# A two-layer decoder trunk: input projections by Strassen's seven products, results passed to the next phase through DRAM

## The chip, the core and the metric

The kernel runs on one core of a Trainium2 chip. The core has five engines that each work through their own list of instructions in order: TensorE (PE) for matrix products, with weight loads (PEld) beside them; VectorE (DVE) and ScalarE (ACT) for elementwise work, both of which read PSUM, the memory that PE writes; GpSimd (POOL) for elementwise work in SBUF, the on-chip memory; and SyncE (SP), which here issues all DMA transfers between DRAM and SBUF. An instruction that waits for a semaphore holds up everything behind it on its engine. The metric is the device time of one execution in microseconds (us).

## The reference, cut to what matters

The input is 1024 tokens of width 1024 in float32. Layer 0 is retention with 4 heads, layer 1 is stick-breaking attention with 8 heads. Both multiply their normed input with wide weight matrices first (`proj`, `kv`), and both end in an output projection, a norm and a residual sum.

```python
u = rms_norm(h, ret_norm_pre[i]); proj = u @ ret_w_in[i]        # 1024 x 1024 @ 1024 x 6144
q, k, v, g = jnp.split(proj, [1024, 2048, 4096], axis=-1)
q = rope(split_heads(q, 4), pos); k = rope(split_heads(k, 4), pos) * 256 ** -0.5
o = retention_chunkwise(q, k, v)          # decayed causal scores, a carried state
o = (o - mu) * lax.rsqrt(var + EPS)       # per head
o = merge_heads(o).astype(h.dtype) * jax.nn.silu(g)
y = o @ ret_w_out[i]
h = h + rms_norm(y, ret_norm_post[i])
kv = rms_norm(h, kv_norm) @ w_kv                                # 1024 x 1024 @ 1024 x 3072
u = rms_norm(h, sb_norm_pre[j]); proj = u @ sb_w_in[j]          # 1024 x 1024 @ 1024 x 3072
o = stick_breaking_attention(q, k_shared, v_shared)             # A = sigmoid(z) * prod(1 - sigmoid(z))
y = (merge_heads(o) * jax.nn.silu(g)) @ sb_w_out[j]
h = h + rms_norm(y, sb_norm_post[j])
```

So the input projections are a 1024 x 1024 matrix times 1024 x 12288 in all.

## The kernel before, in words

Activations are held transposed, channels on the 128 partitions and tokens along the free axis. Every matrix product is done in a format of reduced precision (`F32R`), three times over: an operand is split into a high and a low part, and `mm3` (L114 to L117) adds high x high, high x low and low x high in one PSUM bank. The split (`unit` L107 to L111, `split` L216 and L217) is a copy on ACT into the reduced format and a subtraction on DVE.

`run` (L691) goes through four phases: layer 0 for tokens 0 to 511, layer 0 for tokens 512 to 1023, then layer 1 for each half (`AHead` and `CPair` with t = 0 and 1). Within a phase there are four units (a retention head, or a pair of stick-breaking heads). A unit has three input projections (`proj`, L119: 16 steps of 6 matmuls of 512 columns each, 96 matmuls), its attention (`scores` and `mix`, or `rows` and `mix`), a gate, and its output projection (`outproj`, L145). Weights are loaded and split once per phase, so twice in all. The output of a projection is read by DVE and ACT straight from PSUM and stays in SBUF until its attention uses it. The value and the retention gate come out with tokens on the partitions, because there the activation tile is the stationary operand of the matmul; the queries and keys come out with channels on the partitions.

The order of the work around the change is written out by hand: `merge` (L172) puts the steps of side lists between the steps of a main list, so that score, transpose and mixing matmuls of one unit stand between projection matmuls of the same or the next unit. `merge(H.gproj(), (H.mix(), 3, 0), ...)` in L729 is one such line, `merge(P.kqproj(), (st + [gate], 6, 2), ...)` in L738 another. The norms before the projections are not applied to the activation but to what comes out (`X.cos`, `X.col`, `X.rows`), so the first matmul needs only one tile of x and one of weights. A planning tool then orders instructions on each engine by their dependencies and hands out the buffers.

The seam between layers is spread in the same way: the post-norm of one half (`a_post`, L421) runs beside the projections of the next half, and the last unit's output projection stands beside the loads for the next phase.

Of the kernel before, what the change touches and what calls it, by code (L numbers as in the profile page):

```python
# [15 lines left out]
D = 1024  # L16
# [4 lines left out]
VD = 512  # L21
# [5 lines left out]
G_PRE, G_POST, G_KV, G_SB, G_SBPOST = range(5)  # L27


@with_exitstack  # L30
def trunk(ctx, tc, xT, wts, gains, trig, ident_in, cols, out):
# [7 lines left out]
    BUFS = dict(xh=8, y=8, tab=2, wraw=3, whl=3, qk=4, v=4, vo=4, oT=4, A=5, sgn=2, AT=3,  # L39
                ko=2, sg=4, row=1, f2=5, acc=2, small=24, col=8, mm=4, z=2, o=2)  # L40
    cnt = [0]

    def S(tag, shape, dt=F32):
        cnt[0] += 1
        return sb.tile([128] + list(shape), dt, tag=tag, name=f"{tag}{cnt[0]}", bufs=BUFS[tag])

# [7 lines left out]
    def hl(tag):  # L54
        return S(tag, [2, 512], F32R)
# [8 lines left out]

# [26 lines left out]
    def unit(idx, gain=None):  # L91

        raw = S("wraw", [1024])
        if idx:
            dma(raw[:], wts[idx])
        else:
            gain = [(0, 512, None), (512, 1024, None)]
            for a, b, _ in gain:
                dma(raw[:, a:b], wts[idx, :, a:b])
        w = S("whl", [2, 1024], F32R)  # L100
        if gain is None:
            pieces = [(0, 1024, None)]
        else:
            pieces = gain
        for a, b, g in pieces:
            if g is None:
                A_.activation(w[:, 0, a:b], raw[:, a:b], AF.Copy)  # L107
                V.tensor_tensor(w[:, 1, a:b], raw[:, a:b], f32(w[:, 0, a:b]), ALU.subtract)  # L108
            else:
                A_.activation(w[:, 0, a:b], raw[:, a:b], AF.Copy, scale=g)  # L110
                V.scalar_tensor_tensor(w[:, 1, a:b], raw[:, a:b], g, f32(w[:, 0, a:b]), ALU.mult, ALU.subtract)  # L111
        return w

    def mm3(p, lh, ll, rh, rl, start, stop):  # L114
        MM(p, lh, rh, start=start, stop=False)  # L115
        MM(p, lh, rl, start=False, stop=False)  # L116
        MM(p, ll, rh, start=False, stop=stop)  # L117

    def proj(base, xh, typ, evac, gain=None):  # L119


        box = {}

        def chunk(j):
            i, half = divmod(j, 2)
            kk, c = divmod(i, 2)
            if j == 0:
                box["b"] = [PS("mm") for _ in range(4)]
            if j % 4 == 0:
                box["w"] = unit(base + kk, gain(kk) if gain else None)  # L130
            w, x, banks = box["w"], xh[i], box["b"]
            for b in (2 * half, 2 * half + 1):
                bl = slice(128 * b, 128 * b + 128)
                if typ == "N":
                    n = slice(512 * c + 128 * b, 512 * c + 128 * b + 128)
                    mm3(banks[b][:], w[:, 0, n], w[:, 1, n], x[:, 0, :], x[:, 1, :], i == 0, i == 7)
                else:
                    n = slice(512 * c, 512 * c + 512)
                    mm3(banks[b][:], x[:, 0, bl], x[:, 1, bl], w[:, 0, n], w[:, 1, n], i == 0, i == 7)
            if j == 15:  # L140
                evac(banks)

        return [lambda j=j: chunk(j) for j in range(16)]

    def outproj(base, oT, y, first, acc=None, tag="mm"):  # L145

        box = {}

        def chunk(j):
            c, half = divmod(j, 2)  # L150
            ng, b = divmod(c, 2)
            if j % 4 == 0:
                box["w"] = unit(base + ng)
# [6 lines left out]
            if half == 0:  # L160
                return
# [672 lines left out]
```

## Time and profile before

| | us |
|---|---|
| Time, median of 3 runs | 1819.01 (1818.63 to 1819.77) |
| The profiled execution's own time | 1819.82 |
| Its span, first to last instruction | 1818.0 |
| PE busy | 1767.5 (97%), 8290 matmuls |
| DVE busy | 1038.1 (57%) |
| ACT busy | 724.1 (40%) |
| POOL busy | 308.6 (17%) |
| DMA | 208.09 MB, mean 114 GB/s |

A row of the profile's groups reads: line, engine, operation, output tile and input tiles by the program's names, shape, number of instructions, then after the bar the time that they were busy and the mean of one in nanoseconds, then the idle time of that engine ahead of them and what ended it. Matmuls overlap: the next one starts before the last one's recorded end, so the duration of one (about 390 ns for 512 columns) is longer than the pace at which they follow each other, and the pace is read from the start times in the timeline. The table of waits says which engine waited for which instruction, how long in total, how often, and how long at most. In a table of windows, each stretch of time has the busy time of each engine with the number of instructions, and the clock that was granted to PE (1.00 is full).

### The profile page before, as it was taken

To read this page: it belongs to the slowest core of one execution; us is meant where nothing else is said; L and a number is where in the kernel's file an instruction comes from. 1 tells how busy PE (TensorE), PEld (TensorE's weight loads), DVE (VectorE), ACT (ScalarE), POOL (GpSimd) and SP (SyncE) were. 2 spreads that over 40 slices of the span, in tenths; PEclk is the share of its full clock that TensorE was granted. 3 is DMA by queue.
4 is the path that set the end of the run, shared out by engine and by line. 5 is a ranking of instruction groups with operands and counts; after the bars stand their busy time and mean duration, and the time that the engine had idled before them with its cause. 6 is when DMAs were issued, how large, how long until landed. Compare 5 with 4: busy or idle time off the path is not lost.

```text
span 1818.0 us, 21852 instructions
## 1 busy us (share of the span) xinstructions
PE 1767.5 (97%) x8290; PEld 1466.5 (81%) x8290; DVE 1038.1 (57%) x1588; ACT 724.1 (40%) x1288; POOL 308.6 (17%) x376
## 2 busy tenths in 40 slices
PE   7999999999899999999999999999998999999987
PEld 6888888888788888888877888888876887887876
DVE  7363454564945363545596465556586446756665
ACT  4343323353333232323454343443444434444441
POOL 4110010113431010111122120201212012101123
PEclk9999999999999999999999999999999999999999
DMA  5222222343362232243364423354244232222321
GB/s 175 82 94 92 93 82 92 108 158 105 136 212 93 70 105 92 83 147 108 116 245 172 140 72 127 115 180 133 99 133 134 87 105 93 92 82 91 108 79 49
DMA packets 66376, 208.09 MB, mean 114 GB/s; under 512 B 7520, under 2 KB 9696, under 8 KB 66272
## 3 DMA queue, kind: packets, MB, share of 16 engines
q1 hardware_dynamic: 66272, 206.70, 33.9%
q8 instruction: 65, 1.06, 0.2%
q14 instruction: 39, 0.32, 0.1%
HBM read 173.12 MB, written 33.55 MB: 114 GB/s over the span
## 4 chain that ended last, share of the span: by engine, by line
PE 71%; issue 17%; DVE 7%; POOL 2%; DMA 2%; ACT 1%; SPq 0%; POOLq 0%; DVEq 0%; ACTq 0%
PE pmm L115 19%; PE pmm L117 19%; PE pmm L116 19%; PE po L117 3%; PE po L116 3%; PE po L115 3%; DVE sgn L550 2%; DMA tab<-h 1%; DVE whl L111 1%; PE pz L117 1%; PE pz L116 1%; PE pz L415 1%; PE pz L115 1%; PE pz L575 1%; DVE A L551 1%
## 5 line engine op out<-in xcount | busy, mean ns | idle before, releaser
L108 DVE TENSOR_TENSOR whl<-wraw,whl 128x1024 fp32r<-128x1024 f32 (+1 forms) x158 | 196.6, 1246 | 217.6 <-ACT whl L107 217.3
L115 PE MATMUL pmm<-xh,whl 128*128 128x512 f32 x768 | 308.3, 401 | 11.5 <-ACT whl L107 7.3
L115 PE MATMUL pmm<-whl,xh 128*128 128x512 f32 x768 | 302.1, 394 | 4.1 <-DVE v L308 2.7
L117 PE MATMUL pmm<-xh,whl 128*128 128x512 f32 x768 | 301.9, 393 | 0.7 <-DVE whl L108 0.7
L116 PE MATMUL pmm<-xh,whl 128*128 128x512 f32 x768 | 300.9, 392 | 0.0
L116 PE MATMUL pmm<-whl,xh 128*128 128x512 f32 x768 | 300.3, 391 | 0.0
L117 PE MATMUL pmm<-whl,xh 128*128 128x512 f32 x768 | 300.3, 391 | 0.0
L107 ACT ACTIVATE whl<-wraw 128x1024 fp32r<-128x1024 f32 (+1 forms) x158 | 165.3, 1047 | 237.9 <-PE pmm L117 225.6
L111 DVE SCALAR_TENSOR_TENSOR whl<-wraw,gn,whl 128x256 fp32r<-128x256 f32 (+1 forms) x256 | 153.2, 639 | 103.5 <-ACT whl L110 103.0
L110 ACT ACTIVATE whl<-wraw,gn 128x256 fp32r<-128x256 f32 (+1 forms) x256 | 143.7, 608 | 148.7 <-PE pmm L117 111.0
L115 PEld LDWEIGHTS pmm<-xh,whl 128*128 128x128 f32 x768 | 145.3, 189 | 41.4 <-ACT whl L107 7.3
L115 PEld LDWEIGHTS pmm<-whl,xh 128*128 128x128 f32 x768 | 144.9, 189 | 34.1 <-DVE v L308 2.9
L117 PEld LDWEIGHTS pmm<-xh,whl 128*128 128x128 f32 x768 | 144.8, 189 | 33.5 <-DVE whl L108 1.7
L117 PEld LDWEIGHTS pmm<-whl,xh 128*128 128x128 f32 x768 | 144.7, 188 | 30.8
L116 PEld LDWEIGHTS pmm<-whl,xh 128*128 128x128 f32 x768 | 145.0, 189 | 28.3
L116 PEld LDWEIGHTS pmm<-xh,whl 128*128 128x128 f32 x768 | 145.3, 189 | 26.6
L548 POOL TENSOR_SCALAR_AFFINE_SELECT sgn<-sgn 128x128 f32<-128x128 f32 x64 | 24.9, 389 | 638.8 <-ACT sgn L543 603.0
L115 PE MATMUL pmm<-oT,whl 128*128 128x512 f32 x336 | 132.9, 395 | 0.0
L117 PE MATMUL pmm<-oT,whl 128*128 128x512 f32 x336 | 131.5, 391 | 0.0
L116 PE MATMUL pmm<-oT,whl 128*128 128x512 f32 x336 | 131.4, 391 | 0.0
L550 DVE TENSOR_TENSOR_SCAN sgn<-sgn 128x128 f32<-128x128 f32 (+3 forms) x64 | 92.7, 1448 | 58.8 <-POOL sgn L548 58.8
L191 POOL TENSOR_TENSOR acc<-acc,f 128x512 f32<-128x512 f32 x49 | 74.4, 1522 | 147.5 <-ACT f L190 146.6
(182 smaller groups left out, 2822.5 us busy)
## 6 DMA issues: line engine op xcount, KB each, us to landing
wraw<-in_wts_dram SPq DMA_DIRECT2D x254, 512.0 KB, 3.3
xh<-hh SPq DMA_DIRECT2D x16, 512.0 KB, 3.7
v<-v SPq DMA_DIRECT2D x16, 512.0 KB, 3.2
vo<-v SPq DMA_DIRECT2D x32, 256.0 KB, 3.2
st<-ko SPq DMA_DIRECT2D x8, 512.0 KB, 3.6
vo<-in_xT_dram SPq DMA_DIRECT2D x16, 256.0 KB, 5.1
ko<-st SPq DMA_DIRECT2D x8, 512.0 KB, 3.9
h<-y SPq DMA_DIRECT2D x16, 256.0 KB, 2.7
```

Source lines behind the costliest of these rows:

```text
L107: A_.activation(w[:, 0, a:b], raw[:, a:b], AF.Copy)
L108: V.tensor_tensor(w[:, 1, a:b], raw[:, a:b], f32(w[:, 0, a:b]), ALU.subtract)
L110: A_.activation(w[:, 0, a:b], raw[:, a:b], AF.Copy, scale=g)
L111: V.scalar_tensor_tensor(w[:, 1, a:b], raw[:, a:b], g, f32(w[:, 0, a:b]), ALU.mult, ALU.subtract)
L115: MM(p, lh, rh, start=start, stop=False)
L116: MM(p, lh, rl, start=False, stop=False)
L117: MM(p, ll, rh, start=False, stop=stop)
L191: G.tensor_tensor(acc[:], acc[:], t[:], ALU.add)
L415: nc.tensor.transpose(pt[:, 128 * e:128 * e + 128], on[:, 128 * e:128 * e + 128], ident[:])
L548: G.affine_select(n[:, dg], n[:, dg], [[-1, 128]], ALU.is_gt, 1.0, base=0, channel_multiplier=1)
L550: V.tensor_tensor_scan(n[:, :W][:, ::-1], n[:, :W][:, ::-1], n[:, :W][:, ::-1], 1.0, ALU.mult, ALU.bypass)
L551: V.tensor_tensor(a[:, :W - 1], a[:, :W - 1], n[:, 1:W], ALU.mult)
```

## The change

The four phases become five stages in a row. (1) All of layer 0's input projections, over all 1024 tokens. (2) Retention of the four heads, with the output projection of the head before between its steps. (3) The norms and the residual sum for both halves of the tokens. (4) All of layer 1's input projections. (5) Stick-breaking attention of the four pairs, with the output projection of the pair before between its steps, and the end. What a projection gives goes to DRAM and is loaded again by the attention stage.

The projections are done in blocks. The activation matrix (channels by tokens) is cut into 2 x 2 blocks of 512 channels by 512 tokens; for every 256 output columns, the weights are cut into 2 x 2 blocks of 512 channels by 128 columns. Seven products of sums of such blocks, in the Winograd form of Strassen's algorithm, replace the eight plain ones: `XOps` makes the seven activation operands, `Pair` makes the seven weight operands (`one` and `two` split one or two blocks with one copy on ACT and one subtraction on DVE, 512 or 1024 wide) and runs the products `p1` to `p7`, 12 matmuls of 512 columns each. `project` runs `p1` and `p2` of four pairs first, beside the preparation of the operands that need the second half of the tokens (`second`), then `p5`, `p6`, `p3`, `p7` and `p4` of these four, and then the other pairs whole. A `Pair` covers both halves of the tokens, and there are 24 of them in each layer. The sums need a normed activation, so the norm now stands ahead of the first product. Every projection now comes out with channels on the partitions, and the values are transposed on PE (`PutV`).

The core of the diff:

```diff
+NB, NHALF = 46, 16
...
-def trunk(ctx, tc, xT, wts, gains, trig, ident_in, cols, out):
+def trunk(ctx, tc, xT, wp, wo, gains, trig, ident_in, cols, out):
-    BUFS = dict(xh=8, y=8, tab=2, wraw=3, whl=3, qk=4, v=4, vo=4, oT=4, A=5, sgn=2, AT=3,
-                ko=2, sg=4, row=1, f2=5, acc=2, small=24, col=8, mm=4, z=2, o=2)
+    BUFS = dict(b=NB, h=NHALF, small=24, col=8, mm=4, z=2, o=2)
...
-    def proj(base, xh, typ, evac, gain=None):
...
+    class XOps:
+        def put(self, name, kt, src):
+            x = self.o[name][kt] = hl("x" + name)
+            split((x[:, 0, :], x[:, 1, :]), src)
+        def first(self, kt):
+            self.put("B11", kt, self.src[kt][:, 0, :])
+            self.put("B21", kt, self.src[4 + kt][:, 0, :])
+        def second(self, kt):
+            a, b = self.src[kt], self.src[4 + kt]
+            b11, b12, b21, b22 = a[:, 0, :], a[:, 1, :], b[:, 0, :], b[:, 1, :]
+            t1 = N("t1", [512])
+            V.tensor_tensor(t1[:], b12, b11, ALU.subtract)
+            self.put("T1", kt, t1[:])
+            V.tensor_tensor(b11, b22, t1[:], ALU.subtract)
+            self.put("T2", kt, b11)
+            self.put("B22", kt, b22)
+            G.tensor_tensor(b12, b22, b12, ALU.subtract)
+            self.put("T3", kt, b12)
+            G.tensor_tensor(b21, b21, b11, ALU.subtract)
+            self.put("T4", kt, b21)
+    class Pair:
+        def prep_s12(self):
+            r0, r1 = self.raw
+            s = N("s", [2, 4, 128])
+            V.tensor_tensor(s[:, 0], r0[:, 1], r1[:, 1], ALU.add)
+            V.tensor_tensor(s[:, 1], s[:, 0], r0[:, 0], ALU.subtract)
+            self.s2 = s
+            self.two(("S1", "S2"), s[:])
...
+        def p1(self, tag="mm"):
+            self.al = PS(tag)
+            self.mul(self.al, "A11", "B11", True)
+            self.c1 = self.copy(self.al, "c")
+        def p2(self, tag="mm"):
+            p = PS(tag)
+            self.mul(p, "A12", "B21", True)
+            self.consume(0, 0, self.plus(self.c1, p))
+        def p5(self, tag="mm"):
+            self.be = PS(tag)
+            self.mul(self.be, "S1", "T1", True)
+            self.c5 = self.copy(self.be, "c")
+        def p6(self):
+            self.mul(self.al, "S2", "T2", False)
+            self.c2 = self.copy(self.al, "c")
+        def p3(self):
+            self.mul(self.be, "S4", "B22", False)
+            self.consume(0, 1, self.plus(self.c2, self.be))
+        def p7(self):
+            self.mul(self.al, "S3", "T3", False)
+            self.consume(1, 1, self.plus(self.c5, self.al))
+        def p4(self):
+            self.mul(self.al, "A22", "T4", False)
+            self.consume(1, 0, self.al[:])
+        def steps(self):
+            return [self.p1, self.p5, self.p6, self.p3, self.p7, self.p2, self.p4]
+    def project(pairs, nfirst, second):
+        first = []
+        for i, p in enumerate(pairs[:nfirst]):
+            tag = "mm" if i < 4 else "z"
+            if i == 0:
+                p.prep_early()
+            first += [lambda p=p, tag=tag: p.p1(tag), lambda p=p: p.p2("o")]
+            if i + 1 < nfirst:
+                first.insert(2 * i, pairs[i + 1].prep_early)
+        merge(first, (second, 2, 0))
...
+        for i in range(nfirst, len(pairs)):
+            merge(pairs[i].steps(), (pairs[i + 1].preps() if i + 1 < len(pairs) else [], 0, 1))
...
+                if all((e, t) in self.c for e in range(4)):
+                    for b in range(4):
+                        pt = PS("z")
+                        for e in range(4):
+                            nc.tensor.transpose(pt[:, 128 * e:128 * e + 128],
+                                                self.c[e, t][:, 128 * b:128 * b + 128], ident[:])
+                        self.finish(4 * t + b, pt)
...
+        def load(self):
+            h, t = self.h, self.t
+            self.q, self.k, self.v, self.sg = [], [], [], []
+            for d in range(2):
+                x = hl("k")
+                dma(flat(x), k_d[h][t][d][:])
...
     def run():
-        phases = [("A", 0), ("A", 1), ("C", 0), ("C", 1)]
...
+        X = XOps(xs)
+        stats, norm = x_norm(0)
+        late_constants()
+        for s in stats:
+            s()
+        for kt in range(4):
+            norm[kt]()
+            norm[4 + kt]()
+            X.first(kt)
+        stats, norm = x_norm(1)
+        second = stats + [lambda: [dma(tab[i][:], trig[i]) for i in range(2)]]
+        for kt in range(4):
+            second += [norm[kt], norm[4 + kt], lambda kt=kt, X=X: X.second(kt)]
...
+        project(pairs, 4, second)
+        for h in range(NH):
+            r0, r1 = Ret(h, 0, oT[0], state), Ret(h, 1, oT[1], state)
+            st = [r0.load] + r0.steps()
+            st1 = r1.steps()
+            st = st[:13] + [r1.load] + st[13:] + st1
+            merge(st, (prev, 0, 0))
+            O = Out(4 * h, oT, y, h == 0)
+            prev = O.steps()
...
+        for s in O.half(0, accs[0]):
+            s()
+        post, norm = ret_post(0, y, accs[0], xs2)
+        side = post
+        for kt in range(4):
+            side = side + [norm[kt], norm[4 + kt], lambda kt=kt: X2.first(kt)]
+        merge(O.half(1, accs[1]), (side, 0, 0))
+        post, norm = ret_post(1, y, accs[1], xs2)
+        second = post
+        for kt in range(4):
+            second = second + [norm[kt], norm[4 + kt], lambda kt=kt: X2.second(kt)]
...
+        project(pairs, 4, second)
+        for p in range(NPAIR):
+            hs = [Stick(p, hh, oT) for hh in range(2)]
+            for s in hs:
+                st += [s.load] + s.rows(0) + s.mix(0) + s.rows(1) + s.mix(1)
+            merge(st, (prev, 0, 0))
+            O = Out(16 + 4 * p, oT, y, p == 0)
+            prev = O.steps()
+        last(O, y)
```

`ret_post` does for one half what `a_post` did (norm, residual sum, sum of squares), and returns a `norm` step for each 128 channels besides. `Ret` and `Stick` hold the steps of retention and of stick-breaking attention as they were, with loads of their inputs ahead of them (`load`). `Out` is the output projection, 12 matmuls per 128 channels and half. `last` is the end of the kernel as `finish` was: the output projection of the last pair, the last norm, the residual sum and the stores.

More of the change, by code (lines that the diff above doesn't have):

```diff
@@ L423, in a_post, with ret_post @@
+    def ret_post(t, y, acc, xs):
         box = {}
@@ L650, in chunk @@
             if c == 0:
[L651 removed]
+                A_.activation(aa, yy, AF.Square)
             else:
[L653 to L667 removed]
```

913 lines of the change are left out of this document (439 added, 474 removed).

## The prediction

> **What bounds the kernel now.** I read the page's busy times first, then the waits of PE, then PE's timeline for its pace.
>
> ```profile
> PE 1767.5 (97%) x8290; PEld 1466.5 (81%) x8290; DVE 1038.1 (57%) x1588; ACT 724.1 (40%) x1288; POOL 308.6 (17%) x376
> ```
> ```profile
> PE pz L575 <- DVE AT L217: 11.2, 6, 3.4
> PE pmm L115 <- ACT whl L107: 7.3, 1, 7.3
> PE pz L575 <- DVE A L551: 4.4, 2, 3.7
> PE pz L115 <- ACT A L544: 3.8, 2, 2.9
> ...
> ```
> ```profile
> 22.70 0.40 PE L115 MATMUL pmm<-xh,whl 128*128 128x512 f32 x1
> 22.94 0.39 PE L116 MATMUL pmm<-xh,whl 128*128 128x512 f32 x1
> 23.17 0.39 PE L117 MATMUL pmm<-xh,whl 128*128 128x512 f32 x1
> 23.39 0.39 PE L115 MATMUL pmm<-xh,whl 128*128 128x512 f32 x1
> ...
> 964.82 0.60 PE L575 MATMUL pz<-ident,A 128*128 128x128 f32 x4
> 965.17 0.48 PE L115 MATMUL pmm<-xh,whl 128*128 128x512 f32 x1
> ```
>
> PE is the bound: 97% busy, and its longest kind of wait adds up to 11.2 us of 1818. VectorE has nearly half of its time free, because its work stands beside matmuls everywhere. A 512-column matmul follows the last every 0.23 us (22.70 to 23.39 is 0.69 for three; I use 0.227); four transposes of 128 columns take 0.35 us (964.82 to 965.17), 0.09 each.
>
> **What PE saves.** Before, the input projections are 48 units of 96 matmuls, 4608. After, 48 pairs of 7 x 12, 4032. The 576 fewer are worth 576 x 0.227 = -131 us. Output projection, scores and mixing keep their number. The values now need 256 transposes, 256 x 0.09 = +23 us (by the rows' duration, 0.60 us for four, it would be +38, the bound above). Net -108. If all else stayed hidden, 1712.
>
> **What covers the rest.** It doesn't stay hidden: the projections, which were the cover of every other chain, now stand in two blocks of their own. I price the seams by VectorE's rows.
>
> ```profile
> L411 DVE TENSOR_TENSOR sgn<-sgn,sg 128x512 f32<-128x512 f32 x32 | 21.2, 684 | 3.4 <-ACT sgn L398 3.2
> L620 DVE SCALAR_TENSOR_TENSOR y<-y,gn,row 128x512 f32<-128x512 f32 x8 | 5.7, 735 | 0.0
> L108 DVE TENSOR_TENSOR whl<-wraw,whl 128x1024 fp32r<-128x1024 f32 x154 | 193.6, 1257 | 217.3 <-ACT whl L107 217.0
> L217 DVE TENSOR_TENSOR qk<-f,qk 128x512 fp32r<-128x512 f32 x64 | 52.3, 831 | 11.5 <-ACT qk L216 10.6
> L207 DVE TENSOR_SCALAR AT<-ident,col 128x128 fp32r<-128x128 f32 x28 | 6.9, 283 | 5.2 <-POOL col L200 4.8 <-PE po L117 0.3
> L208 DVE SCALAR_TENSOR_TENSOR AT<-ident,col,AT 128x128 fp32r<-128x128 f32 x28 | 8.8, 345 | 0.1
> L200 POOL TENSOR_TENSOR col<-small,mhalf 128x4 f32<-128x4 f32 x7 | 9.7, 1387 | 35.3 <-DVE small L198 22.5 <-DVE small L303 12.8
> L191 POOL TENSOR_TENSOR acc<-acc,f 128x512 f32<-128x512 f32 x49 | 74.4, 1522 | 147.5 <-ACT f L190 146.6
> L550 DVE TENSOR_TENSOR_SCAN sgn<-sgn 128x128 f32<-128x128 f32 (+3 forms) x64 | 92.7, 1448 | 58.8 <-POOL sgn L548 58.8
> L551 DVE TENSOR_TENSOR A<-A,sgn 128x127 f32<-128x127 f32 (+3 forms) x64 | 52.6, 822 | 4.3
> ```
> ```profile
> 7.31 0.79 PE L115 MATMUL pmm<-xh,whl 128*128 128x512 f32 x1 [7.31 <-ACT whl L107]
> ```
>
> *The start.* Before, PE begins at 7.31 us, since the norm is applied to the output; with slow first matmuls and two gaps it loses some 11 us. Now all of the first half of x must land (about 10 us), be squared and summed, and a norm row must be made: four small products, POOL 1.39, eight diagonal pieces 4 x (0.28 + 0.35) = 2.5, a product, a copy, 7 us with the hops, so 18. Up to the first `p5`, VectorE in its built order has 16 normings x 0.735 = 11.8, 51 sums and splits of 512 x 0.684 = 34.9, diagonal pieces 2.5, one wide split 1.3: 51 us, with some 10 for waits on POOL and ACT inside the list, so `p5` starts near 79. PE has 8 x 12 matmuls to do by then, 22 us. Loss 57, less the 11: **+47** (bounds 35 and 60).
>
> *Projections in their steady state.* A pair is 84 x 0.227 = 19.1 us of PE. A query or key pair gives VectorE 22 instructions of 512 and 3 of 1024: 22 x 0.684 + 3 x 1.257 = 18.8, just hidden. Without `p1` and `p2` (the first two) it is 13.6 against 16.9: 3.3 lost each. Where a key pair follows a query pair, the third matmul of `p2` waits for a split that stands behind 19 VectorE instructions, about 4 us by their sum, in three heads. With small waits elsewhere **+22** (5 to 40; at the upper end the 0.831 row, which has POOL beside it, holds for all). Values and gates need some 12 us of VectorE and hide.
>
> *Retention* (36 us of PE a head: 108 long matmuls, the scores, 48 transposes) keeps only the output projection of the head before as cover, and head 0 has none: there the chains of norm and gate show, about 13 us. For the later heads, the first output weights are loaded only after the last output matmul of the head before; 3.3 us to land and a split against 2.8 us of scores, 3 us each. **+20** (5 to 45).
>
> *Between the layers.* From the first matmuls of `O.half(1)` to the `p5` of layer 1, VectorE has 148 instructions: 91 of 512 x 0.684 = 62.2, 16 normings 11.8, 32 diagonal pieces 10.0, the rest 4.7: 89 us. Three norm rows can't be covered (products and POOL's 1.39, 2.8 each) and POOL's sums of 1.52 hold it up a little: with the 3.7 before, 109. PE has 192 matmuls in that time, 44 us: 65 lost. Before, this seam and its waits cost about 9: **+56** (40 to 75).
>
> *Stick-breaking.* A head has 22 us of PE. Its chain without cover: rows of the first half 6, their mixing and gate 8, then VectorE's four long rows one after another, about 12 of the 145/8 = 18 us that scans (92.7) and products (52.6) take per head, then mixing 13, with hops 42. Pair 0 has no cover: 2 x 20 lost. The others have 22 us of output projection per head, of which a quarter to a half falls beside PE-bound mixing and not into waits: 50 against 44, six times, 38. Together 78, less 18 that the waits table shows around these tiles before: **+60** (15 to 110).
>
> *The clock.* Two stretches around idle PE, from its timeline and from a table of windows (busy time of PE, PEld, DVE, ACT and POOL with their counts, the granted clock, the DMA share, GB/s):
>
> ```profile
> 968.14 0.39 PE L117 MATMUL pmm<-xh,whl 128*128 128x512 f32 x1
> 971.90 0.66 PE L575 MATMUL pz<-ident,A 128*128 128x128 f32 x2 [3.37 <-DVE AT L217]
> ...
> 1752.19 0.47 PE L575 MATMUL pz<-ident,A 128*128 128x128 f32 x1 [3.66 <-DVE A L551]
> ```
> ```profile
> 960.00:972.00 12.00, 8.63 (x42) 6.83 (x42) 12.00 (x19) 7.43 (x15) 4.99 (x4) 0.94 0.37 113
> 972.00:977.00 5.00, 5.00 (x13) 3.99 (x14) 0.65 (x2) 0.38 (x1) 0.00 (x0) 0.50 0.94 365
> 1740.00:1752.00 12.00, 8.11 (x36) 6.50 (x36) 9.40 (x9) 8.07 (x14) 8.27 (x8) 1.00 0.05 20
> 1752.00:1756.00 4.00, 3.81 (x13) 3.08 (x14) 4.00 (x7) 0.69 (x2) 0.00 (x0) 0.57 0.00 0
> ```
>
> After an idle stretch of 3.37 us PE runs at half clock (0.50 in the window from 972); so it does after the 3.66 us before 1752.19 (0.57). That costs some 2.5 us each time in which PE has work. Of about 19 idle stretches of that length that I count, some five are followed by work that PE bounds and that isn't priced already: **+12** (0 to 50).
>
> *DRAM and the rest.*
>
> ```profile
> q1 hardware_dynamic: 66272, 206.70, 33.9%
> wraw<-in_wts_dram SPq DMA_DIRECT2D x254, 512.0 KB, 3.3
> ko<-k SPq DMA_DIRECT2D x8, 512.0 KB, 4.0
> ```
>
> The results' way through DRAM adds 191 transfers on SP's queue (645 for 454) and 55 MB to 207, at 34% use of the DMA engines before. Loads are issued ahead wherever buffers allow; uncovered, one costs 3 to 4 us (the last two rows: from issue to landing), and those at head boundaries are counted. The end of the kernel keeps its form: 0 (-3 to +15).
>
> **Sum.** -108 + 47 + 22 + 20 + 56 + 60 + 12 = +109 on the profiled execution's 1819.8 (span 1818.0, 1.8 around it; the median is 0.8 below): **1929 us**.
>
> **Rivals.** *The order fills the waits* (faster). The built order places ready matmuls of the output projection and of early products ahead of waiting ones, so the idle stretches that I add up lie beside work. Start, middle and both attention stages are 183 us; if 109 of them (60%) vanish, the kernel is no slower, and with 75% it takes 1792. For it speaks 97% busy before, under the same planning tool. Against it: in the middle 89 us of VectorE stand against 44 of PE, and no order mends that. 0.12.
>
> *VectorE runs at its slower rows.* Where POOL works too, 512 columns took 0.831 and not 0.684. Eight query and key pairs then go to 22.5 us on VectorE, 27 more, and the two seams' 142 instructions of 512 cost 21 more: 1977. The rows with POOL beside them speak for it, PSUM operands at 0.68 against. 0.17.
>
> *The clock falls at each idle stretch.* 19 stretches at 3.4 us (6.8 us at half) are 65, not 12: 1982. The third of these windows speaks for it; that in many stretches PE isn't the bound, against. 0.16. [...]
>
> **How the numbers follow.** The forecast itself, 1880 to 1975 by its likelier bounds, has 0.53; a tie with 1819 has 0.02. Slower is 0.53 + 0.17 + 0.16 = 0.86, faster 0.12. 0.2% (4 us) is about what a measurement can tell from no change. The range 1850 to 2005 takes in both slower rivals and leaves out the faster one.
>
> **What would show it.** PE's count falls by about 320 and its busy share to near 90%; PE idle some 30 us ahead of the first `p5`, some 50 between the layers; VectorE at 9 tenths or more there; waits of transposes of `A` on the product with the scan several us long, 16 times; granted clock below 0.98. Wrong would be: VectorE idle in the seams, PE at 95%, or a long wait of PE on DMA.

## The result, and the profile after

The changed kernel takes 2018.25 us (median of 4 runs, 2017.31 to 2019.07) against 1818.82 us before (1818.13 to 1819.77): a ratio of 1.1096, with a 95% interval of 1.1077 to 1.1115. It is 199 us slower, where 109 were forecast and the range ended at 2005. The sign was right and the size was not.

From the profile's page of the changed kernel, the busy times and three rows of the span in 40 slices (tenths of each slice of 50.4 us; the last row is the granted clock):

```profile
PE 1746.1 (87%) x7970; PEld 1412.9 (70%) x7970; DVE 1178.1 (58%) x1685; ACT 800.2 (40%) x1410; POOL 239.7 (12%) x338
...
PE   3489999999998999994518999999997788999986
...
DVE  5876757667543344444575564655555565657655
...
PEclk9789999999998999997658999999998799999998
```

PE has 320 matmuls fewer and went from 97% busy to 87%. The holes are where the prediction put them: at the start (3, 4), between the layers (4, 5, 1) and in stick-breaking (7, 7, 8, 8). But VectorE's row contradicts it at the second hole: the prediction wanted 9 tenths or more there, and the row has 4, 5, 7. Only the last 40 us ahead of the first product of layer 1 that needs the second half (`p5`) look as forecast. From a table of windows (length; busy time and number for PE, PEld, DVE, ACT and POOL; granted clock, DMA share, GB/s):

```profile
1024.00:1064.20 40.20, 1.45 (x3) 0.62 (x3) 35.31 (x50) 16.53 (x30) 13.97 (x9) 0.50 0.12 39
```

PE's waits in the changed kernel (total, times, longest):

```profile
PE po L102 <- ACT wh L109: 67.2, 3, 36.0
PE pz L696 <- DVE A L681: 38.9, 35, 3.2
PE pz L145 <- DVE acc L140: 38.3, 3, 22.3
PE pmm L102 <- ACT w L109: 31.2, 3, 13.9
```

Of the first row, 62 us are the two waits for the first `p5`, 26 us at the start and 36 us between the layers. The longest waits of the third and the fourth row lie between the layers too: PE waited 22.3 us from 925 us on for a sum of squares, and 13.9 us from 989 us on for weights. The next longest, 13.0 and 11.0 us, are at the start.

To compare places, I cut PE's timeline into stages and count in each the work, which is its matmuls at the pace of full clock (227 ns from start to start at 512 columns, 174 at 384, 119 at 256, 88 at 128: medians of the trace, but at 128 columns and below, where waits stand between many of them, a value from the lower third). What a stage takes beyond its work is its loss. For the kernel before, the work is 1724 us of the span of 1818.0, so 94 are lost. After, the work is 1616: 108 less, as forecast. All of the miss is in the loss. The table ends with the last matmul; the span has 8.5 us more, for the rest of the last norm and the stores.

| stage of the changed kernel | from, us | length | work | loss | forecast loss |
|---|---|---|---|---|---|
| start, to the first `p5` | 0 | 89.6 | 23.4 | 66 | 57 |
| rest of layer 0's projections | 89.6 | 486.3 | 447.1 | 39 | |
| retention | 575.9 | 348.8 | 319.0 | 30 | |
| between the layers, to `p5` | 924.8 | 139.4 | 24.3 | 115 | 65 |
| rest of layer 1's projections | 1064.2 | 458.3 | 447.1 | 11 | |
| stick-breaking | 1522.5 | 414.9 | 306.4 | 108 | 78 |
| the end | 1937.4 | 69.8 | 48.8 | 21 | |

The three stages with a forecast of their own miss by 9, 50 and 30 us. That is 89 us, the distance from 1929 to 2018; what the other places miss by cancels. The projections and retention together lose 80 us; of what the kernel before loses, some 35 us have no other place than its own projections and attention (94 less the 38 that the prediction took off at the three seams, less about 21 for the end), so they grew by about 45, where 54 were forecast (22, 20 and 12 for the clock). The end, with the 8.5 us behind the last matmul, loses about 8 us more than before, where 0 was forecast.

The largest miss is between the layers. SyncE's queue there, from the changed kernel's timeline (start, duration, and what is issued):

```profile
923.60 0.33 SPq L70 DMA_DIRECT2D h<-y  x1
924.01 0.38 SPq L70 DMA_DIRECT2D f<-in_xT_dram  x1
927.50 0.33 SPq L70 DMA_DIRECT2D h<-y  x1
927.92 0.38 SPq L70 DMA_DIRECT2D f<-in_xT_dram  x1
932.69 0.33 SPq L70 DMA_DIRECT2D h<-y  x1
933.11 0.38 SPq L70 DMA_DIRECT2D f<-in_xT_dram  x1
```

And VectorE's rows for the sums that use those loads, with the idle time ahead of each in brackets:

```profile
935.87 0.69 DVE L610 TENSOR_TENSOR y<-y,f 128x512 f32<-128x512 f32 x1 [6.89 <-DMA f<-in_xT_dram]
...
945.09 0.69 DVE L610 TENSOR_TENSOR y<-y,f 128x512 f32<-128x512 f32 x1 [7.00 <-DMA f<-in_xT_dram]
...
1002.00 0.69 DVE L610 TENSOR_TENSOR y<-y,f 128x512 f32<-128x512 f32 x1 [9.59 <-DMA f<-in_xT_dram]
```

In `ret_post` each channel loads its piece of x (`f`), adds it to y and stores the sum (`h`). But for the first of each half, each load is issued right behind the store of the channel before (0.4 us; in one place 1.4 us, with two loads of weights between), never earlier. The store waits for the sum, and the sum for its own load: so load, sum, store and the next load form one chain, at some 4.8 us a channel (eight stores from 912.5 to 945.8 us), while VectorE idles most of the time. In the first half, a load goes out 0.4 us behind the store ahead of it, whether that store came 3.9 us after the one before or 5.6: the queue takes its transfers in order here, and a store that waits holds up the load behind it.

### The profile page after: what moved, and what is told of

Read it like the earlier page. It is cut to its first block, busy times and chain, and to the rows that moved or that the text cites. A ratio compares the mean times of both kernels' runs of the same rounds, so it can differ in the third digit from the quotient of the medians.

```text
span 2015.7 us, 21886 instructions
## 1 busy us (share of the span) xinstructions
PE 1746.1 (87%) x7970; PEld 1412.9 (70%) x7970; DVE 1178.1 (58%) x1685; ACT 800.2 (40%) x1410; POOL 239.7 (12%) x338
## 5 line engine op out<-in xcount | busy, mean ns | idle before, releaser
L102 PE MATMUL pmm<-xT,wh 128*128 128x512 f32 x704 | 276.0, 392 | 0.0
L103 PE MATMUL pmm<-xT,wh 128*128 128x512 f32 x704 | 275.9, 392 | 0.0
L104 PE MATMUL pmm<-xT,wl 128*128 128x512 f32 x704 | 275.6, 392 | 0.0
L102 PE MATMUL pmm<-oT,wh 128*128 128x512 f32 (+1 forms) x544 | 213.6, 393 | 3.2 <-ACT wh L109 3.1
L104 PE MATMUL pmm<-oT,wl 128*128 128x512 f32 (+1 forms) x544 | 208.3, 387 | 5.7 <-DVE wl L110 5.7
L103 PE MATMUL pmm<-oT,wh 128*128 128x512 f32 (+1 forms) x544 | 210.4, 387 | 0.0
L102 PEld LDWEIGHTS pmm<-xT,wh 128*128 128x128 f32 x704 | 133.7, 190 | 28.6 <-ACT c L288 0.4
L103 PEld LDWEIGHTS pmm<-xT,wh 128*128 128x128 f32 x704 | 133.3, 189 | 27.8
L104 PEld LDWEIGHTS pmm<-xT,wl 128*128 128x128 f32 x704 | 133.0, 189 | 27.8
L110 DVE TENSOR_TENSOR wl<-s,wh 128x1024 fp32r<-128x1024 f32 x96 | 118.5, 1235 | 48.3 <-ACT wh L109 48.1
L102 PE MATMUL pmm<-xB,wh 128*128 128x512 f32 x320 | 127.7, 399 | 9.2 <-ACT wh L109 9.2
L104 PE MATMUL pmm<-xB,wl 128*128 128x512 f32 x320 | 127.3, 398 | 1.2 <-DVE wl L110 1.2
L103 PE MATMUL pmm<-xB,wh 128*128 128x512 f32 x320 | 126.6, 396 | 0.0
L102 PEld LDWEIGHTS pmm<-oT,wh 128*128 128x128 f32 x544 | 105.2, 193 | 21.7 <-ACT wh L109 4.7
L103 PEld LDWEIGHTS pmm<-oT,wh 128*128 128x128 f32 x544 | 105.4, 194 | 17.2
```

Source lines behind the costliest of these rows:

```text
L102: MM(p, lh, rh, start=start, stop=False, **kw)
L103: MM(p, lh, rl, start=False, stop=False, **kw)
L104: MM(p, ll, rh, start=False, stop=stop, **kw)
L110: V.tensor_tensor(dst[1], src, f32(dst[0]), ALU.subtract)
```

## The experiments

All times are medians; the changed kernel stands at 2018.25 us. The kernel before, run beside each group, had medians of 1816.9 to 1818.4 us, so differences of 2 us between groups mean nothing.

### Loads ahead of the stores

```diff
 def ret_post(t, y, acc, xs):
     box = {}
+    raws = [N("f", [512]) for _ in range(8)]
+    for c in range(8):
+        dma(raws[c][:], xT[128 * c:128 * c + 128, tk(t)])
...
     def step(c):
-        raw = N("f", [512])
-        dma(raw[:], xT[128 * c:128 * c + 128, tk(t)])
+        raw = raws[c]
```

> Theory A, the queue: between the layers each of the 16 loads of x stands on SP's queue behind the store of the channel before it, so the post-norm goes at the pace of load, sum, store, load (8 channels in 35 us, 912.5 to 946, and again in 39 us, 982 to 1021). With the eight loads of a half issued ahead, a half needs about 14 us (8 x 0.74 and 4 x 0.68 us on VectorE, 4 sums and 4 square sums of 1.27 us on POOL): 30 to 45 us fall away, 1973 to 1988 us. Theory B, VectorE's own 89 us set the seam, as the prediction had it: at most 5 us, not under 2013 us.

Measured: 1982.23 us (1980.02 to 1985.58), ratio 1.091 (1.089 to 1.0929). 36 us fell away. SyncE's queue in this run:

```profile
874.75 4.63 SPq L70 DMA_DIRECT2D f<-in_xT_dram  x8
913.91 17.14 SPq L70 DMA_DIRECT2D h<-y  x8
931.14 3.80 SPq L70 DMA_DIRECT2D f<-in_xT_dram  x8
```

Windows over the post-norm of the first half, the changed kernel ahead and this run behind (length, then busy time and number for PE, PEld, DVE, ACT, POOL, then clock, DMA share, GB/s):

```profile
912.00:947.00 35.00, 13.15 (x59) 10.55 (x57) 13.74 (x20) 7.10 (x13) 11.88 (x10) 0.76 0.32 109
```
```profile
911.00:933.00 22.00, 14.24 (x63) 11.27 (x61) 21.72 (x22) 7.66 (x13) 16.28 (x10) 0.90 0.28 107
```

The same chain takes 22 us in place of 35, and VectorE, which had 13.7 us to do in 35, is now busy for 21.7 of 22. So theory A holds, and behind it stands what the prediction had put first: with the queue out of the way, VectorE is busy all through this stretch. Part of that isn't work: the mean of its instructions went from 0.69 to 0.99 us, for a reason shown below (sums of operands). The seam's loss is now 17 us ahead of the first product and 52 from there to `p5`, and retention's end, into which the seam reaches, loses 11 more than before the edit: 80 us, where 65 were forecast.

### Eight products in the same stages

```diff
         def second(self, kt):
-            a, b = self.src[kt], self.src[4 + kt]
...
-            self.put("T4", kt, b21)
+            self.put("B12", kt, self.src[kt][:, 1, :])
+            self.put("B22", kt, self.src[4 + kt][:, 1, :])
...
-        def prep_s12(self):
...
-        def prep_s43(self):
...
+    def part(self, i, t, k, tag="mm"):
+        if k == 0:
+            self.p = PS(tag)
+        self.mul(self.p, f"A{i + 1}{k + 1}", f"B{k + 1}{t + 1}", k == 0)
+        if k:
+            self.consume(i, t, self.p[:] if (i, t) == (1, 0) else self.copy(self.p, "c")[:])
```

> The same five stages and the same way through DRAM, with the eight plain block products in place of the seven, and no sums of blocks. Theory A: the seven products do save 576 x 0.227 = 131 us of PE, and their price is the longer operand lists in the two seams (20 VectorE instructions of 0.68 us and the stalls beside 8 POOL sums, some 20 us a seam) and the waits at the key pairs (17 us): 2018 + 131 - 57 = 2092 us (2070 to 2115). Theory B: the sums eat most of the saving: under 2050 us. Both leave the stages themselves as the larger loss: far above 1819.

Measured: 2052.77 us (2051.06 to 2054.2), ratio 1.1295 (1.1279 to 1.1312). Seven products save 34.5 us against eight; that lies between the two theories, close to theory B's bound. By stages, the projections' work is 2 x 512.5 us here against 2 x 447.1: the saving on PE is there in full, 131 us. But eight lose 24 us less at the start (42 for 66), 34 less in the rest of layer 0's projections (5.5 for 39.2) and 37 less between the layers (78 for 115). So the operand sums, and the longer lists that PE waits for, give back 96 us of 131. And with eight products, without any sum of blocks, the same five stages are 236 us slower than the kernel before (the transposes of the values, 23 us by the prediction's estimate, are in that). So the order of the stages makes the kernel slow, and Strassen's form takes 34.5 us off.

### A value pair between query and key

```diff
-            pairs += [Pair(6 * h, X, put_rope(h, q_d, tab)), Pair(6 * h + 1, X, put_rope(h, k_d, tab)),
-                      Pair(6 * h + 2, X, v.half(0)), Pair(6 * h + 3, X, v.half(2)),
+            pairs += [Pair(6 * h, X, put_rope(h, q_d, tab)), Pair(6 * h + 2, X, v.half(0)),
+                      Pair(6 * h + 1, X, put_rope(h, k_d, tab)), Pair(6 * h + 3, X, v.half(2)),
```

> In layer 0 a value pair stands between the query pair and the key pair of each head. Theory A: the three waits of 2.7, 3.8 and 2.7 us at the key pairs and the half-clock stretches behind them (13 to 15 matmuls at 0.43 us, some 2.8 us each) come from 19 VectorE instructions of the query pair's rotation ahead of the split that PE wants: they vanish, 14 to 18 us, 2000 to 2004 us. Theory B: VectorE stays behind anyway, and the wait moves to another pair: 0 to 4 us.

Measured: 2004.35 us (2002.29 to 2007.62), ratio 1.1031 (1.1013 to 1.1049): 14 us, as theory A has it. Layer 0's projections lose 27.6 us in place of 39.2. One of the three places in the changed kernel, from PE's timeline and a table of windows:

```profile
247.87 0.80 PE L102 MATMUL pmm<-xB,wh 128*128 128x512 f32 x1 [2.68 <-ACT wh L109]
```
```profile
247.80:254.00 6.20, 5.91 (x13) 4.22 (x14) 5.61 (x7) 2.17 (x5) 1.59 (x1) 0.50 0.22 84
254.00:260.00 6.00, 6.00 (x27) 4.96 (x27) 1.29 (x2) 1.12 (x2) 0.00 (x0) 1.00 0.93 327
```

A wait of 2.68 us costs as much again behind it: 13 matmuls in 6.2 us where 27 go into 6.0. The prediction had the wait (about 4 us, in three heads) and not its second half. It counted idle stretches of some 3.4 us (3.37 and 3.66 in its two examples); here the clock stood at 0.50 behind a recorded wait of 2.68 us, so a count of the longer ones alone is too low.

### Sums of operands from POOL to VectorE

```diff
-    G.tensor_tensor(b12, b22, b12, ALU.subtract)
+    V.tensor_tensor(b12, b22, b12, ALU.subtract)
...
-    G.tensor_tensor(b21, b21, b11, ALU.subtract)
+    V.tensor_tensor(b21, b21, b11, ALU.subtract)
```

> The 16 sums of operands that POOL makes (T3 and T4) go to VectorE. Theory A: beside each POOL sum one VectorE instruction took about 1.75 us for 0.69, so VectorE loses 1.06 us and would take 0.6 for the sum itself: 16 x 0.46 = 7 us faster, 2011 us (2006 to 2014). Theory B: VectorE's list sets both seams and gets 16 x 0.6 = 10 us longer: 2028 us.

Measured: 2011.44 us (2009.4 to 2017.4), ratio 1.1066 (1.1045 to 1.1087): 7 us, on theory A's number. But the profiled run doesn't show it where theory A puts it. That run is 4.6 us faster; the start is 0.2 us shorter, the seam between the layers 0.9, and 2.8 us lie in stick-breaking, which has none of these sums. So part of the 7 us may be variation between runs. What the rows do show is that POOL's sums hold VectorE. Two neighbours in the changed kernel's timeline, on POOL and on VectorE:

```profile
1033.72 1.65 POOL L208 TENSOR_TENSOR xs<-xs,xs 128x512 f32<-128x512 f32 x1 [0.63 <-DVE xs L202]
```
```profile
1034.16 1.76 DVE L623 TENSOR_TENSOR xs<-y,row 128x512 f32<-128x512 f32 x1
```

And two of VectorE's groups in the 35 us ahead of the `p5` of layer 1, the changed kernel first and then this run (number, busy time and mean of one):

```profile
L623 DVE TENSOR_TENSOR xs<-y,row 128x512 f32<-128x512 f32 x8 | 8.6, 1084 | 0.0
L202 DVE TENSOR_TENSOR xs<-xs,t 128x512 f32<-128x512 f32 x4 | 5.6, 1390 | 0.0
```
```profile
L623 DVE TENSOR_TENSOR xs<-y,row 128x512 f32<-128x512 f32 x8 | 5.3, 692 | 0.0
L202 DVE TENSOR_TENSOR xs<-xs,t 128x512 f32<-128x512 f32 x4 | 2.8, 692 | 0.0
```

An instruction on two SBUF tiles that took 0.69 us alone took up to 1.76 beside a sum on POOL. The one shown ended 0.55 us after POOL's; beside each of the eight sums that POOL makes between 1031 and 1058 us there is one such instruction, of 1.37 to 1.76 us, and it ends 0.54 to 0.56 us after POOL's. I read this as: it was held until POOL's sum was done. The held instruction shown lost 1.07 us, and a sum on VectorE takes 0.6 us from start to start, so work that is given to POOL to relieve VectorE can take more of VectorE's time than doing it there. PE's wait for the `p5` of layer 1 fell from 36.0 to 34.4 us, 1.6 where eight sums at 0.46 would give 3.7.

### The first stick-breaking pair side by side

```diff
+    if p == 0:
+        a, b = hs
+        st += [a.load] + a.rows(0) + [b.load]
+        for u, w in ((a.mix(0), b.rows(0)), (a.rows(1), b.mix(0)), (a.mix(1), b.rows(1))):
+            st += [f for i in range(max(len(u), len(w))) for f in u[i:i + 1] + w[i:i + 1]]
+        st += b.mix(1)
```

> The two heads of the first stick-breaking pair run beside each other: the scores of the second beside the mixing of the first, and so on. Theory A: this pair takes 92.6 us (1522.4 to 1615) for 44 us of PE since nothing covers the chain of a head, 45 us; beside each other the two chains take about 65 us: 20 to 35 us fall away, 1983 to 1998 us. Theory B: VectorE's and ACT's order or the PSUM buffers line the chains up all the same: at most 5 us.

Measured: 2009.97 us (2009.18 to 2010.72), ratio 1.106 (1.1044 to 1.1077): 8 us, between the theories. In the profiled run the pair is 86.3 us long in place of 91.8. PE's waits in this pair, the changed kernel (1522 to 1615 us) and this run (1520 to 1608 us):

```profile
PE pz L696 <- DVE A L681: 14.1, 10, 3.2
```
```profile
PE pz L696 <- DVE A L681: 12.1, 7, 3.2
```

The wait of the transposes for the product with the scan is nearly as long as it was. If a transpose that waits at the head of PE's list holds the other head's scores behind it, that would explain why a second chain beside the first covers little, but no run here puts its instructions ahead of the waiting ones.

### The clock in that pair

```diff
     for tb in range(t0, 4):
+        if self.pr == 0 and i == 0:
+            pd = PS("mm")
+            for _ in range(5):
+                MM(pd[:], onesr[:], self.K[t][:, 0, :], start=True, stop=True)
         nc.tensor.transpose(...)
```

> In the first stick-breaking pair, five matmuls of 512 columns whose result nobody reads stand ahead of each of the 16 transposes that wait for a product with the scan: 80 x 0.227 = 18 us of work in waits of 14 us. Theory A, the clock: the pair has 44 us of work at full clock and takes 92.6 at a granted clock of 0.78; with PE kept busy in the waits the clock stays up, and the pair gets shorter although it holds more work: 2 to 10 us faster, 2008 to 2016 us, and a granted clock above 0.9 there. Theory B, the chain through ACT, POOL and VectorE sets the pair, and the half clock lies beside it: no gain, 0 to 18 us slower, 2018 to 2036 us.

Measured: 2016.19 us (2014.11 to 2020.63), ratio 1.109 (1.1072 to 1.1108): no change. A window over the pair in the changed kernel, and with 80 matmuls more (there the pair begins 2 us later, so the window holds the end of a projection too):

```profile
1522.40:1615.00 92.60, 68.19 (x295) 51.91 (x294) 56.47 (x71) 34.88 (x80) 14.76 (x32) 0.78 0.46 163
```
```profile
1522.00:1615.00 93.00, 78.28 (x368) 60.90 (x367) 56.79 (x71) 35.48 (x80) 13.89 (x32) 0.89 0.48 170
```

The clock rose from 0.78 to 0.89, PE did 18 us of work more, and from its first score to its last mixing matmul the pair takes 92.0 us for 91.8. So PE's amount of work doesn't set this pair: it has room for 18 us, and the chain over the other engines is what is left. That the half clock costs nothing here is likely, but not shown: the added matmuls could cost what the clock gained.

### Scores in banks of their own

```diff
-    p = PS("z")
+    p = PS("mm")
     mm3(p[:, :ww], Q[:, 0, ql], Q[:, 1, ql], KK[:, 0, :ww], KK[:, 1, :ww], True, True)
```

> The scores of stick-breaking attention get PSUM banks of the pool of four that the output projection uses, and no longer share two with the transposes. Theory A: PE's 10.4 us of waits of scores for a sigmoid come from the two banks; the later rows' scores run ahead, and 8 to 25 us fall away over 8 heads, 1993 to 2010 us. Theory B: VectorE's scans and the hops set each head, the scores only wait elsewhere: within 4 us.

Measured: 2009.58 us (2008.61 to 2011.31), ratio 1.1051 (1.1035 to 1.1068): 9 us, the lower end of theory A. The stage loses 102 us in place of 108, and the transposes' waits for the product with the scan grew from 38.9 to 44.9 us: the two banks were a small part of the stage's loss.

### Stick-breaking without its scan

```diff
-    V.tensor_tensor_scan(n[:, :W][:, ::-1], n[:, :W][:, ::-1], n[:, :W][:, ::-1], 1.0, ALU.mult, ALU.bypass)
-    V.tensor_tensor(a[:, :W - 1], a[:, :W - 1], n[:, 1:W], ALU.mult)
```

> The changed kernel without the scan and the product with it in stick-breaking attention (128 VectorE instructions, 145 us, left out). Theory A, the chain of a head with these 18 us in it sets the stage: of its 108 us of loss some 75 fall away (pair 0 by 15 us a head, the six others by 8), 1943 us (1925 to 1965). Theory B, PSUM banks, hops and the output projection's place in PE's order set it: at most 25 us, over 1993 us.

Measured: 1961.11 us (1959.66 to 1963.19), ratio 1.0787 (1.0771 to 1.0804): 57 us fell away. The stage in the changed kernel and in this run:

```profile
1522.50:1937.40 414.90, 360.22 (x1717) 281.78 (x1716) 259.25 (x329) 161.31 (x347) 57.50 (x128) 0.93 0.35 120
```
```profile
1520.80:1878.20 357.40, 336.75 (x1716) 272.21 (x1715) 126.54 (x200) 161.93 (x347) 39.07 (x128) 0.98 0.40 140
```

VectorE is busy for 259 of 415 us, so it doesn't bound the stage by its load. But 57 of the 108 us of loss go with these 128 instructions, so the chain in which they stand is what PE waits for. The other 51 us are put down to the rest of the chain (sigmoids, selections, copies and hops); no run takes those apart.

### Each result stored twice

```diff
+    def dma2(dst, src, w=1024):
+        dma(dst, src)
+        dma(twin[...][:, 0:w], src)
...
-    dma(dst[h][t][d][:], flat(r))
+    dma2(dst[h][t][d][:], flat(r))
```

> Each result of a projection is stored a second time, to a place that nobody reads: 160 further transfers and some 67 MB on SP's queue. Theory A, the way through DRAM is hidden, as the prediction had it: within 4 us of 2018. Theory B, the queue or the DMA engines are near their limit in the projection stages: 15 us or more on top, 2033 us.

Measured: 2063.3 us (2061.6 to 2067.93), ratio 1.1352 (1.1332 to 1.1373): 45 us more, 32 in layer 1's projections and 13 in layer 0's, so theory A falls. (The trace has 192 further transfers and 84 MB more, not 160 and 67.) Layer 1's projections as a whole, changed kernel and this run:

```profile
1064.00:1522.00 458.00, 455.13 (x2046) 373.58 (x2047) 256.30 (x347) 252.28 (x445) 0.00 (x0) 0.99 0.40 147
```
```profile
1075.00:1565.00 490.00, 463.38 (x2046) 378.48 (x2047) 259.38 (x347) 251.33 (x445) 0.00 (x0) 0.97 0.58 219
```

By their mean share, 0.58, the DMA engines have room, but the mean hides bursts. In the changed kernel the eight stores of a group of values go out one behind the other, with the next weights behind them:

```profile
1240.55 11.20 SPq L70 DMA_DIRECT2D sv<-r  x8
1251.84 1.35 SPq L70 DMA_DIRECT2D wr<-in_wp_dram  x2
```

With every store doubled, the weights of such a place go out later than PE wants them, and into engines that are full. From this run's windows (a DMA share of 1.02: all engines busy) and timeline:

```profile
1270.00:1288.00 18.00, 18.00 (x84) 14.89 (x84) 8.15 (x11) 6.54 (x11) 0.00 (x0) 1.00 1.02 388
```

```profile
1282.01 2.42 SPq L70 DMA_DIRECT2D wr<-in_wp_dram  x2
```
```profile
1294.29 0.80 PE L102 MATMUL pmm<-xB,w 128*128 128x512 f32 x1 [4.99 <-ACT w L109]
```

PE waited 4.99 us there for the weights' split; there are four such waits in this layer, of 4.4 to 8.4 us. So the way through DRAM costs little as it is (layer 1's projections lose 11 us from all causes), but its bursts leave little room ahead of the next weights. Whether their place behind the stores on the one queue or the full DMA engines make them late, this run doesn't separate.

### The five edits together

The edits of the loads, the value pair, the operand sums, the side-by-side pair and the score banks in one kernel.

> The five edits that each made the kernel faster, together: loads ahead, the value pair between query and key, operand sums on VectorE, the first stick-breaking pair side by side, scores in the pool of four banks. If their places are apart, the gains add: 36 + 14 + 7 + 8 + 9 = 74 us, 1944 us (1935 to 1955). If VectorE takes over in the seam between the layers as soon as the loads are gone, the gains overlap there: above 1955 us.

Measured: 1944.63 us (1941.78 to 1944.88), ratio 1.0691 (1.0673 to 1.0709). The five gains add, to within 1 us. By stage, the profiled run loses 38 us less between the layers and at retention's end, 20 less in stick-breaking, 11 less in layer 0's projections and 3 less at the start. That the sum agrees so closely is in part luck, since the gain of the operand sums alone wasn't found at its place.

### All sums of both seams on VectorE

```diff
-def sumsq(acc, src, c, eng=nc.gpsimd):
+def sumsq(acc, src, c, eng=nc.vector):
...
-            (V if c % 2 else G).tensor_tensor(yy, yy, raw[:], ALU.add)
+            V.tensor_tensor(yy, yy, raw[:], ALU.add)
...
-            sumsq(box["acc"], yy, c, nc.vector if c % 2 else nc.gpsimd)
+            sumsq(box["acc"], yy, c)
...
-                sumsq(box["acc"], xs[c][:, t, :], c, nc.gpsimd if t else nc.vector)
+                sumsq(box["acc"], xs[c][:, t, :], c)
```

> As the five edits together, and POOL's residual sums and sums of squares in both seams on VectorE as well, 30 instructions. Theory A, VectorE sets the seams and loses 1.06 us beside each POOL sum but takes 0.6 us for it: 30 x 0.46 = 14 us less, and the hops between the two engines go: 10 to 20 us below the five edits. Theory B, VectorE's list gets 18 us longer and the seams with it: 10 to 18 us above them.

Measured: 1928.61 us (1923.92 to 1929.88), ratio 1.0603 (1.0584 to 1.0622): 16 us below the five edits, as theory A has it (the edit moves 35 instructions, not 30). In the profiled run 10 us of that lie between the layers and at retention's end, 4 at the start. This is the fastest form that the experiments gave, and it is still 6% slower than the kernel before. From its page:

```profile
PE 1719.7 (89%) x7970; PEld 1399.5 (73%) x7970; DVE 1180.7 (61%) x1736; ACT 798.8 (41%) x1410; POOL 166.6 (9%) x287
```

Its loss is 59 us at the start, 67 between the layers and 91 in stick-breaking. These need other work beside them, and the five stages have too little there.

### Eight products in the mended kernel

The eight products as above, in the kernel with all sums on VectorE.

> The eight plain block products again, now in the kernel with the five edits and all sums on VectorE (1928.6 us with seven). In the changed kernel the eight cost 34.5 us more than the seven, where PE alone has 131 us more to do: the seven lost 97 us to their operand sums in the two seams and to the waits of layer 0's projections. Theory A: the edits mended about half of those places, so eight now cost 50 to 75 us more, 1979 to 2004 us. Theory B: VectorE's list in the seams is what it was, and eight cost at most 40 us more, under 1969 us.

Measured: 1985.44 us (1985.19 to 1986.91), ratio 1.0918 (1.0892 to 1.0944): eight cost 57 us more than seven. Of the 131 us that PE saves, 57 arrive now instead of 34.5. Eight lose 25 us less at the start, 19 less in layer 0's projections and about 36 less between the layers.

## Why the prediction was wrong

- **What PE saves, net -108: right.** The work fell from 1724 to 1616 us, and the eight products show the 131 us of the projections by themselves.
- **Between the layers, +56: the step that failed.** The loss grew by 106 us, outside the term's own bounds of 40 to 75. The prediction counted VectorE's 148 instructions, 89 us, and let everything else fit beside them, with three norm rows and POOL's sums as the only holdups. That count was right: from about the first matmuls of the last output projection's second half (902 us) to the `p5` the trace has 148 instructions on VectorE, busy for 94 us. But they took 162 us and not 109. The step that failed is the overlap: the prediction took the loads as issued ahead and didn't walk SyncE's queue. It wrote of the DMAs that loads are issued ahead wherever buffers allow; in this seam a load can't be issued ahead, since the store of the channel before waits in front of it. The loads ahead took 36 us of the 50 that were missing. Most of the rest goes with POOL's sums: with all sums on VectorE, the seam and retention's end lost 10 us less than with the five edits, by the end of the holding, of POOL's slower rows and of hops together. In that kernel the seam itself loses 67 us, about the 65 that were forecast. The prediction's sign, VectorE at 9 tenths or more in the seam, was the right test, and it failed: VectorE was at 4 to 7, and near 9 in the last 40 us alone.
- **Stick-breaking, +60: right mechanism, two terms too small.** The first pair's heads take 45 and 47 us against 22 us of PE each, a loss of 23 and 25 where 20 was taken. The six others take 52 to 56 us against 40 to 45, a loss of 8 to 13 where 6.3 was taken. Together 108 us of loss instead of 78. The chain with the scan is the larger part of the cause as forecast (57 us by leaving it out), and the output projection hid less of it than assumed.
- **Start, +47: nearly right.** The first `p5` came at 89.6 us, not at 79. The 10 us allowed for waits on POOL and ACT were too few by about 10; with all sums on VectorE it comes at 82.4.
- **Projections, retention, clock: +54 in sum, about 45 measured.** The waits at the key pairs were found in the built order and were there, at three places; the half clock behind each (0.50 to 0.53 granted, over 3.3 to 6.7 us) belonged to them.
- **The way through DRAM, 0: right in the projections, and without room to spare.** The stores twice show how close the next weights stand behind the bursts of stores. The forecast's 34% use of the DMA engines was a mean, and such a mean hides bursts: in the changed kernel they are all busy from 1252 to 1256 us (a share of 1.00), right behind eight stores.
- **What was to show it.** PE's count fell by 320 as said, its share to 87% for near 90, the clock to 0.935 for under 0.98; PE's waits for the first `p5` were 26 us and 36 us. The transposes' waits for the product with the scan came 35 times and not 16, and none was over 3.2 us: many short waits make up that stage's loss, each too short to stand out.
- **The rivals.** The order didn't fill the waits. VectorE at its slower rows was true as a mechanism, but the mean of 0.831 us hid it: most rows take 0.69 and some up to 1.76 (in the kernel before, that row has a median of 0.683 and a longest of 1.78), and what decides is whether POOL makes a sum at that moment (the 16 rows of layer 1's norm take 0.68 to 1.76 us in the changed kernel, and 0.681 to 0.685 with all sums on VectorE). By the medians it was worth at most 7 us for the operand sums and 16 for the others, not 48. The clock at half for 6.8 us is there in the kernel before (0.50 from 496.0 to 502.8 us and from 970.5 to 977.3), and so is a stretch of 3.4 us (1752.1 to 1755.5); but behind an idle stretch of 2.82 us there, which ends at 493.6 us, the clock stood at 1.00. The added matmuls show that PE had room where the chain of other engines set the pace. The prediction let the third of its windows speak for that rival; that window has the clock at 1.00, and it is the fourth, at 0.57, that does.
- **The range.** It ended 13 us too early, since it left out a queue that no term looked at. That the total came this near has some luck in it: the projections, retention and the clock came out 9 us under their terms, and the end about 8 us over.

## What to carry to other kernels

Before work that was spread out is gathered into stages, walk every queue through the seam in its built order, the one that issues the transfers too: a load behind a store that waits for a result made a chain of them here, at some 4.8 us a channel, and no count of VectorE's work showed it. A load for which buffers are free is not yet a load that goes out early. A saving on the bound engine is worth what is left after the operands it asks for: here 131 us of matmuls gave 34.5 us, since the sums fell where nothing covered them. If VectorE is late, a sum given to POOL beside it can make it later: here one held instruction lost 1.07 us where the sum itself takes VectorE 0.6.

## What the runs showed of the hardware that I had not expected

Beside each of POOL's eight operand sums ahead of layer 1's `p5` (1.27 to 1.77 us each), one of VectorE's instructions took 1.37 to 1.76 us for 0.69, and ended 0.54 to 0.56 us after POOL's. Moving 35 of POOL's sums to VectorE made the kernel 16 us faster, on top of the five edits; for the 16 operand sums alone it was 7 us by the median, which the profiled run doesn't show at their place. Where doubled stores filled the DMA engines (a share of 1.02 from 1270 to 1288 us), the last three stores of that group of values took the queue 1.11 to 1.12 us each to issue, against 0.32 in the changed kernel (the median of its 32 stores of layer 1's values). The clock fell to half behind a recorded wait of 2.68 us and stayed there for 6.2 us. And extra matmuls in PE's waits raised the granted clock from 0.78 to 0.89, and the time stayed as it was.
